# Dilated attention in steps by head, six PSUM banks for a layer's last products, and later sums for the conditions

## The chip, the cores and the metric

The kernel runs on one core of a Trainium2 chip. The metric is the time of one execution on the device in microseconds, taken as the median of several runs. The core has TensorE (PE; PEld is its weight load), VectorE (DVE), ScalarE (ACT), GpSimd (POOL), and SyncE (SP), which issues the DMAs. Each engine executes its instructions in the order in which they were written, and waits in that order too. TensorE writes its products into PSUM, which the kernel divides into eight banks.

## The reference, cut to what matters

A transformer of two blocks with two layers each works on 256 latent tokens of width 1024 (and, in the first block, on 256 context tokens beside them), in float32. Shift, scale and gate vectors of all layers come from condition vectors by `silu(c) @ ada_w + ada_b`. The first block's layer 0 is a retention mixer and a SwiGLU feed-forward on all 512 tokens, its layer 1 a neighbourhood attention and a feed-forward. Each layer of the second block is feed-forward, hybrid mixer, feed-forward:

```python
f = swiglu_2(modulate_2(rmsnorm(h, ln_ffn1[l]), sh1, sc1), ffn1_wg[l], ffn1_wu[l], ffn1_wd[l])
h = h + MACARON_WEIGHT * gt1[:, None, :] * f
u = modulate_2(rmsnorm(h, ln_mix[l]), sh2, sc2)
m = hybrid_mixer(u, ...)
...
def hybrid_mixer(...):
    o_a = gated_delta_rule(q, k, v, g, beta)      # 8 heads of 128, after a convolution
    y_a = o_a @ w_a
    for window, dilation in ((128, 1), (512, 4), (2048, 16)):
        o_p, lse_p = dilated_window_branch(qd, kd, vd, slopes, window, dilation)   # 12 heads of 64
    o_b = sum of the branches' outputs, weighted by softmax over their log-denominators
    y_b = o_b @ w_b
    merged = sigmoid(gate_a) * y_a + sigmoid(gate_b) * y_b
    return merged @ w_o
```

## The kernel before, in words

Every product with a weight matrix is made in three float32r matmuls: the weight tile `w_raw` arrives by DMA, ACT copies its high part (`w_hi`, line `hi`), DVE subtracts it for the low part (`w_lo`), and PE adds high times high, high times low and low times high (`ah`, `al`, `hh`, `hl`, `v_hi`, `v_lo` are the two parts of the activations). A product on 256 tokens has matmuls of 256 columns, one of layer 0 of 512.

The order of all instructions on all engines is fixed when the program is built: it is the order in which the Python code issues them. The code keeps an estimated clock for each engine (`Times`); `b.clock` is PE's. A **side** is a generator that runs beside the main products: after each group of matmuls `b.run` calls `pump`, which lets sides take steps. A side that must be done is run to its end by `finish`, with nothing of the main products between its steps. The sides in a hybrid mixer are the convolution, the delta-rule recurrence ("chain", `delta`, tiles `d_...`), the decays, the condition vectors (`ada_gen`, on DVE) and the dilated attention (`dilated`).

`dilated` treats six pairs of heads through `b.pipeline`, a list of stages. Before the change `first` makes the scores of two heads (8 matmuls from `da_k`, `da_q` into two `ps_tr` banks) and for each head adds the slope (DVE, `da_dist`), takes two maxima (DVE, `da_st`) and two exponentials (ACT); `normalize` multiplies by the number of branches that see a key and sums (DVE, `da_mult`), inverts (DVE) and scales (ACT), again for both heads; `second(0)` and `second(1)` transpose one head each (3 matmuls) and copy it out (ACT: `n_t`, `da_pt`); `third` multiplies with the values (12 matmuls on `sb`) and splits the result (`ah` on ACT, `al` on DVE). The score tile is `n_a` in the trace. A stage is taken when its input and bank are estimated to be there. A stage's fourth entry, where it is given, is a number of microseconds: the stage is then taken only when DVE's estimated work reaches no further than that past PE's clock. The mixer writes its second gate into the memory of the values (`sb`), so the evacuation `gate_b(i)` calls `da.finish()` for i of 1 and above.

There are six PSUM banks for products (`ps_acc` four, `ps_mm` two) and two for the rest (`ps_tr`). `bank(many)` gives one of the six, whichever is free first, if `many` is true, and one of the two of `ps_mm` otherwise. In layer 0 the products `outp` of the retention and `down` of the feed-forward add to the residual `h` in their evacuation on DVE; where they are the layer's last, the evacuation also prepares the following norm (subtraction of `n_piv` on DVE, squares on ACT, sums on POOL, at last sums over partitions by PE into `ps_tr` and `ps_acc`).

`ada_gen` adds up a condition's product on DVE (`ada_acc`, 8 steps for each half), turns and reduces it (`ada_t`, `ada_part`) and puts it on `pending`; `reduce_one` then makes one small matmul with `fold` into `ps_tr` and two DVE operations. The vectors are also forced by `need`, when a product asks for them.

All helpers record one line, L75, so the tiles' names tell the operations apart. The line numbers that the change touches: `ada_gen` 434, `outp` 1269, the layer's `ffn` 1349 with `down` at 1381, and `dilated` 2093.

## Time and profile before

| | |
|---|---|
| time, median of 3 runs (lowest to highest) | 2873.59 us (2870.81 to 2875.27) |
| profiled execution: time / span | 2875.96 us / 2874.1 us |
| mean granted TensorE clock | 0.977 of full |
| busy: PE / PEld / DVE / ACT / POOL | 97% / 89% / 73% / 46% / 10% |
| chain that ended last | PE 82%, DVE 8%, ACT 4%, issue 3% |

The profile shows one execution. "Busy" is the time in which an engine executes; what it waited for is inferred from semaphores. The granted clock of a stretch is a mean: 1.0 is 2.4 GHz, and the lower of its two levels, 1.2 GHz, is 0.5. The chain is followed back from the last instruction, at each step to what released it. 1560 to 1880 us is about the first hybrid mixer, 2310 to 2630 the second; layer 0 of the first block ends at about 890.

### The profile page before, as it was taken

How to read it: one execution, taken by the hardware profiler on the slowest of the kernel's cores; microseconds unless marked ns; L12 is line 12 of the kernel's file. 1: busy time of each engine (PE TensorE's matmuls, PEld its weight loads, DVE VectorE, ACT ScalarE, POOL GpSimd, SP SyncE). 2: the span in 40 equal slices, each digit the busy share in tenths (PEclk: the TensorE clock that was granted, in tenths of full speed). 3: DMA queues.
4: the chain of work that ended last, by engine and by line, in shares of the span. 5: the costliest groups of instructions: out<-in, count | busy, mean ns of one | idle time of the engine just before them, and what ended most of it. 6: DMA issues, size and time to landing. Idle time of an engine off the chain costs nothing.

```text
span 2874.1 us, 49237 instructions
## 1 busy us (share of the span) xinstructions
PE 2776.9 (97%) x19349; PEld 2548.0 (89%) x19349; DVE 2097.7 (73%) x3396; ACT 1322.0 (46%) x2318; POOL 290.0 (10%) x363
## 2 busy tenths in 40 slices
PE   8999998999998998998999989999999999999999
PEld 4878887888877778998999989999999998899999
DVE  5888886887877776787877777788565577676754
ACT  4433323422224544444445665554454456655543
POOL 0000002000002100001002123210010022130100
PEclk9999998999998998998999999999999999999999
DMA  7444441576755543775886533458566654324564
GB/s 232 155 129 144 141 154 63 190 234 211 239 180 144 122 149 117 253 255 157 267 261 199 155 92 115 147 173 273 186 181 184 186 172 118 89 82 153 179 183 133
DMA packets 433245, 488.34 MB, mean 170 GB/s; under 512 B 34651, under 2 KB 362301, under 8 KB 433013
## 3 DMA queue, kind: packets, MB, share of 16 engines
q1 hardware_dynamic: 431972, 484.59, 54.1%
q8 instruction: 152, 2.49, 0.4%
q10 hardware_dynamic: 1040, 0.60, 0.1%
q14 instruction: 81, 0.66, 0.1%
HBM read 484.07 MB, written 1.05 MB: 169 GB/s over the span
## 4 chain that ended last, share of the span: by engine, by line
PE 82%; DVE 8%; ACT 4%; issue 3%; DMA 1%; SPq 1%; POOL 1%; ACTq 0%; DVEq 0%; POOLq 0%
PE ps_acc L75 46%; PE ps_mm L75 32%; PE ps_tr L75 4%; DVE w_lo L75 2%; ACT w_hi L75 2%; DVE n_t L75 1%; DMA ada_w<-ada_w 1%; ACT n_a L75 1%; DVE n_a L75 1%; DVE h L75 1%; DVE al L75 1%; SPq L75 1%; DVE ada_acc L75 0%; DVE da_st L75 0%; ACT ah L75 0%
## 5 line engine op out<-in xcount | busy, mean ns | idle before, releaser
L75 DVE TENSOR_TENSOR w_lo<-w_raw,w_hi 128x1024 fp32r<-128x1024 f32 (+1 forms) x672 | 816.5, 1226 | 426.5 <-ACT w_hi L75 420.8
L75 ACT ACTIVATE w_hi<-w_raw 128x1024 fp32r<-128x1024 f32 (+2 forms) x686 | 699.7, 1032 | 490.3 <-PE ps_acc L75 233.9
L75 PE MATMUL ps_mm<-ah,w_hi 128*128 128x256 f32 (+1 forms) x2288 | 707.0, 309 | 8.1 <-DVE q_lo L75 3.0
L75 PE MATMUL ps_mm<-ah,w_lo 128*128 128x256 f32 (+1 forms) x2288 | 680.8, 298 | 4.0 <-POOL w_lo L75 2.3
L75 PE MATMUL ps_mm<-al,w_hi 128*128 128x256 f32 (+1 forms) x2288 | 681.7, 298 | 0.2
L75 PEld LDWEIGHTS ps_mm<-ah,w_hi 128*128 128x128 f32 x2288 | 434.9, 190 | 31.4 <-issue 11.1
L75 PEld LDWEIGHTS ps_mm<-ah,w_lo 128*128 128x128 f32 x2288 | 435.2, 190 | 18.9 <-POOL w_lo L75 3.4
L75 PEld LDWEIGHTS ps_mm<-al,w_hi 128*128 128x128 f32 x2288 | 435.7, 190 | 12.4 <-DVE al L75 1.0
L75 PE MATMUL ps_acc<-ah,w_hi 128*128 128x256 f32 (+2 forms) x1440 | 436.4, 303 | 2.3 <-ACT w_hi L75 2.3
L75 PE MATMUL ps_acc<-ah,w_lo 128*128 128x256 f32 (+2 forms) x1440 | 433.5, 301 | 1.4 <-DVE w_lo L75 1.3
L75 PE MATMUL ps_acc<-al,w_hi 128*128 128x256 f32 (+2 forms) x1440 | 433.3, 301 | 0.0
L75 DVE SCALAR_TENSOR_TENSOR ada_acc<-ada_w,cact,ada_acc 128x512 f32<-128x512 f32 x476 | 354.4, 759 | 16.8 <-DMA ada_w<-ada_w 11.8
L75 PEld LDWEIGHTS ps_acc<-ah,w_lo 128*128 128x128 f32 x1440 | 274.7, 191 | 12.5 <-DVE w_lo L75 2.6
L75 PEld LDWEIGHTS ps_acc<-ah,w_hi 128*128 128x128 f32 x1440 | 274.5, 191 | 12.2 <-ACT w_hi L75 2.5
L75 PEld LDWEIGHTS ps_acc<-al,w_hi 128*128 128x128 f32 x1440 | 274.8, 191 | 9.6
L75 PE MATMUL ps_acc<-hh,w_hi 128*128 128x256 f32 (+1 forms) x866 | 255.5, 295 | 0.0
L75 PE MATMUL ps_acc<-hh,w_lo 128*128 128x256 f32 (+1 forms) x866 | 255.2, 295 | 0.0
L75 PE MATMUL ps_acc<-hl,w_hi 128*128 128x256 f32 (+1 forms) x866 | 254.9, 294 | 0.0
L75 POOL TENSOR_TENSOR n_a<-n_a 128x512 f32<-128x512 f32 (+1 forms) x28 | 40.4, 1444 | 1292.6 <-ACT n_a L75 1292.1
L75 PEld LDWEIGHTS ps_acc<-hh,w_hi 128*128 128x128 f32 x866 | 163.2, 188 | 4.4
L75 PEld LDWEIGHTS ps_acc<-hl,w_hi 128*128 128x128 f32 x866 | 163.2, 188 | 4.4
L75 PEld LDWEIGHTS ps_acc<-hh,w_lo 128*128 128x128 f32 x866 | 163.0, 188 | 4.4
(391 smaller groups left out, 4368.5 us busy)
## 6 DMA issues: line engine op xcount, KB each, us to landing
ada_w<-ada_w SPq DMA_DIRECT2D x448, 256.0 KB
w_raw<-w_in SPq DMA_DIRECT2D x132, 512.0 KB
w_raw<-ffn_w SPq DMA_DIRECT2D x128, 512.0 KB
w_raw<-ffn_wg SPq DMA_DIRECT2D x88, 512.0 KB
w_raw<-ffn_wu SPq DMA_DIRECT2D x88, 512.0 KB
w_raw<-ffn_wd SPq DMA_DIRECT2D x80, 512.0 KB
w_raw<-ret_w_in SPq DMA_DIRECT2D x48, 512.0 KB
w_raw<-na_w_qkv SPq DMA_DIRECT2D x24, 512.0 KB
```

Source lines behind the costliest of these rows:

```text
L75: r = f(*args, **kw)
```

## The change

Three edits. (1) `ada_gen` takes the reduction of a finished condition only when its input is estimated to be written, not only when a `ps_tr` bank is free. (2) The last retention product and the last part of layer 0's feed-forward may use all six banks. (3) In `dilated`, `first` ends with the slope; maxima and exponentials are a stage `soft(i)` for each head, and `normalize(i)` is one for each head. `first`, `soft` and `normalize` carry 1.0 us as the fourth entry, so that they are taken only when DVE is estimated at most 1.0 us behind PE. The limits are the same ones with the new stage numbers.

```diff
@@ ada_gen
                         while len(self.pending) > 1:
-                            if not self.force and self.free("ps_tr", self.BANKS["tr"]) > self.clock:
+                            when = max(self.free("ps_tr", self.BANKS["tr"]),
+                                       self.times.when(self.times.written, self.pending[0][2]))
+                            if not self.force and when > self.clock:
                                 yield WAIT
@@ outp
-            return b.gemm_b(self.o[h], ..., 512, self.residual(gates, norms), ks=4, many=norms is None)
+            return b.gemm_b(self.o[h], ..., 512, self.residual(gates, norms), ks=4, many=True)
@@ ffn
-                           self.residual(gates, self.norms if part == NP - 1 else None), ks=2 * (f1 - f0), many=part < NP - 1))
+                           self.residual(gates, self.norms if part == NP - 1 else None), ks=2 * (f1 - f0), many=True))
@@ dilated
                 nc.vector.scalar_tensor_tensor(s, dist, slope, ps[:, :384], op0=OP.mult, op1=OP.add)
-                st = P.tile([128, 2, 4], F32, name="da_st", bufs=4)
+                S[n].append((s, P.tile([128, 2, 4], F32, name="da_st", bufs=4)))
+
+        def soft(i):
+            def f(n):
+                s, st = S[n][i]
                 for t, (a, z) in enumerate(segs):
                     nc.vector.tensor_reduce(st[:, t, 0:1], s[:, a:z], axis=AX.X, op=OP.max, negate=True)
                 for t, (a, z) in enumerate(segs):
                     nc.scalar.activation(s[:, a:z], s[:, a:z], AF.Exp, bias=st[:, t, 0:1])
-                S[n].append((s, st))
-
-        def normalize(n):
-            for s, st in S[n]:
+            return f
+
+        def normalize(i):
+            def f(n):
+                s, st = S[n][i]
...
-        stages = ((first, lambda: "tr2", (3, lambda: 2)), (normalize, None, None), (second(0), tr, (4, lambda: 1)), (second(1), tr, None),
-                  (third, tr, None))
+        stages = ((first, lambda: "tr2", (6, lambda: 2), 1.0), (soft(0), None, None, 1.0), (soft(1), None, None, 1.0),
+                  (normalize(0), None, None, 1.0), (normalize(1), None, None, 1.0), (second(0), tr, (7, lambda: 1)),
+                  (second(1), tr, None), (third, tr, None))
```

No instruction is added or removed on any engine; the order changes. Three places follow, each with the rows of the order before and of the order after the change. A row is one instruction (xN: N alike in a row), its outputs and inputs.

ScalarE in the first hybrid mixer, before: exponentials and scalings of `dilated` (`n_a<-n_a,da_st`, two to a head) around copies of weights.

```order
L75 ACTIVATE w_hi<-w_raw 128x1024
L75 ACTIVATE n_a<-n_a,da_st 128x128
L75 ACTIVATE n_a<-n_a,da_st 128x256
L75 ACTIVATE n_a<-n_a,da_st 128x128
L75 ACTIVATE n_a<-n_a,da_st 128x256
L75 ACTIVATE n_a<-n_a,da_st 128x128
L75 ACTIVATE n_a<-n_a,da_st 128x256
L75 ACTIVATE n_a<-n_a,da_st 128x128
L75 ACTIVATE n_a<-n_a,da_st 128x256
L75 ACTIVATE d_XX<-ps_acc 128x256
L75 ACTIVATE cv_x<-ps_mm 128x512
```

The same engine where `dilated` takes its first steps after the change.

```order
L75 ACTIVATE d_t_14769<-ps_acc 128x256
L75 ACTIVATE n_a<-n_a,da_st 128x128
L75 ACTIVATE n_a<-n_a,da_st 128x256
L75 ACTIVATE n_a<-n_a,da_st 128x128
L75 ACTIVATE n_a<-n_a,da_st 128x256
L75 ACTIVATE w_hi<-w_raw 128x1024
L75 ACTIVATE d_XX<-ps_acc 128x256
```

Eight such operations stood between `w_hi` and the chain's `d_XX`; here four stand in a row between a chain copy (`d_t`) and the next `w_hi`.

TensorE in the first hybrid mixer, before, at an end of a pair (`n_t,sb` and `da_pt,sb` are `third`, `ident,n_a` is `second`).

```order
L75 MATMUL ps_tr<-n_t,sb 64x128
L75 MATMUL ps_tr<-da_pt,sb 64x128
L75 MATMUL ps_tr<-ident,n_a 128x128 x3
L75 MATMUL ps_mm<-ah,w_hi 128x256
L75 MATMUL ps_mm<-al,w_hi 128x256
L75 MATMUL ps_mm<-ah,w_lo 128x256
```

TensorE after the change where the evacuation of the second gate forces `dilated` to its end. `da_k,da_q` is `first`.

```order
L75 MATMUL ps_mm<-ah,w_lo 128x256
L75 MATMUL ps_tr<-ident,n_a 128x128 x6
L75 MATMUL ps_tr<-da_k,da_q 128x128 x2
L75 MATMUL ps_tr<-da_k,da_q 128x256 x2
L75 MATMUL ps_tr<-n_t,sb 64x128
L75 MATMUL ps_tr<-da_pt,sb 64x128
```

One or two steps of `dilated` stood between products (`ps_mm`). Now the run goes on behind the last row in the same way through pairs 3, 4 and 5: in all it holds `second` for pairs 2 to 5, `first` for 4 and 5 and `third` for 2 to 5, with no product and no chain step between; in the second hybrid mixer a like run holds `first` for 4 and 5, `second` for 3 to 5 and `third` for 2 to 5. Before, while `dilated` ran, no stretch without a product held half as many matmuls.

VectorE in the last part of layer 0's feed-forward, before: evacuations `h<-ps_mm` of one weight tile's products, the low part of the next weights, and the condition sums.

```order
L75 SCALAR_TENSOR_TENSOR h<-ps_mm,v_lat_0_5_2933,h 128x256
L75 SCALAR_TENSOR_TENSOR h_67<-ps_mm,v_ctx_0_5_3446,h_67 128x256
L75 SCALAR_TENSOR_TENSOR h<-ps_mm,v_lat_0_5_2933,h 128x256
L75 TENSOR_TENSOR h<-h,n_piv 128x512
L75 SCALAR_TENSOR_TENSOR h_67<-ps_mm,v_ctx_0_5_3446,h_67 128x256
L75 TENSOR_TENSOR h_67<-h_67,n_piv 128x512
L75 TENSOR_TENSOR w_lo<-w_raw,w_hi 128x1024
L75 SCALAR_TENSOR_TENSOR ada_acc<-ada_w,cact,ada_acc 128x512 x2
L75 TENSOR_TENSOR w_lo<-w_raw,w_hi 128x1024
```

The same rows after the change (`h_67` is the context's part of the residual in both).

```order
L75 SCALAR_TENSOR_TENSOR h<-ps_acc,v_lat_0_5_2933,h 128x256
L75 SCALAR_TENSOR_TENSOR h_67<-ps_acc,v_ctx_0_5_3446,h_67 128x256
L75 SCALAR_TENSOR_TENSOR h<-ps_acc,v_lat_0_5_2933,h 128x256
L75 TENSOR_TENSOR h<-h,n_piv 128x512
L75 SCALAR_TENSOR_TENSOR h_67<-ps_acc,v_ctx_0_5_3446,h_67 128x256
L75 TENSOR_TENSOR h_67<-h_67,n_piv 128x512
L75 TENSOR_TENSOR w_lo<-w_raw,w_hi 128x1024
L75 SCALAR_TENSOR_TENSOR ada_acc<-ada_w,cact,ada_acc 128x512
L75 TENSOR_TENSOR w_lo<-w_raw,w_hi 128x1024
```

The evacuations read another bank, and one of the two `ada_acc` steps ahead of the next `w_lo` has moved further down.

## Rows read from the trace of the kernel before

**Rows 1.** Page, part 1: busy time of each engine, share of the span, instructions
```profile
PE 2776.9 (97%) x19349; PEld 2548.0 (89%) x19349; DVE 2097.7 (73%) x3396; ACT 1322.0 (46%) x2318; POOL 290.0 (10%) x363
```

**Rows 2.** TensorE's waits, whole span: engine, tile, releaser: us in total, times, longest
```profile
PE ps_acc L75 <- DVE d_MQ L75: 9.7, 2, 4.8
PE ps_mm L75 <- DVE h L75: 9.4, 4, 3.9
...
PE ps_tr L75 <- DVE ada_part L75: 3.2, 3, 2.7
```

**Rows 3.** Stretches: length, busy us (x) of PE, PEld, DVE, ACT, POOL; PEclk, DMA
```profile
860.00:870.00 10.00, 6.12 (x18) 4.68 (x17) 8.25 (x11) 2.21 (x3) 4.88 (x4) 0.66 0.52 160
1610.00:1740.00 130.00, 119.61 (x995) 112.52 (x994) 97.80 (x243) 83.03 (x209) 26.95 (x38) 0.97 0.38 114
1670.00:1680.00 10.00, 5.16 (x28) 4.96 (x27) 6.83 (x24) 5.40 (x13) 1.27 (x2) 0.73 0.18 53
1860.00:1870.00 10.00, 9.05 (x63) 9.00 (x64) 6.40 (x10) 2.43 (x3) 0.57 (x1) 0.83 0.39 130
2360.00:2510.00 150.00, 139.51 (x1169) 132.60 (x1168) 106.05 (x257) 97.15 (x243) 31.38 (x47) 0.98 0.37 110
```

**Rows 4.** Timeline, scores in the first hybrid: start, us, operation, [idle before <-releaser]
```profile
1671.28 1.54 ACT L75 ACTIVATE n_a<-n_a,da_st 128x128 f32<-128x128 f32 x4 [0.82 <-DVE da_st L75]
...
1673.80 1.23 DVE L75 TENSOR_TENSOR w_lo<-w_raw,w_hi 128x1024 fp32r<-128x1024 f32 x1 [1.81 <-ACT w_hi L75]
...
1675.27 0.87 DVE L75 SCALAR_TENSOR_TENSOR d_MQ<-ps_acc,d_st,d_XX 128x256 f32<-128x256 f32 x2
...
1675.81 1.22 PE L75 MATMUL ps_acc<-d_XX,d_t 128*128 128x128 f32 x4 [4.84 <-DVE d_MQ L75]
```

**Rows 5.** Groups on VectorE in 1610 to 1740: xcount | busy us, mean ns
```profile
L75 DVE SCALAR_TENSOR_TENSOR n_a<-n_a,da_mult 128x128 f32<-128x128 f32 (+1 forms) x24 | 8.4, 388 | 0.0
L75 DVE TENSOR_REDUCE da_st<-n_a 128x1 f32<-128x128 f32 (+1 forms) x24 | 7.3, 347 | 0.4
L75 DVE SCALAR_TENSOR_TENSOR n_a<-da_dist,ps_tr 128x384 f32<-128x384 f32 x12 | 6.6, 547 | 0.0
```

**Rows 6.** Groups on ScalarE in the same stretch
```profile
L75 ACT ACTIVATE n_a<-n_a,da_st 128x128 f32<-128x128 f32 (+1 forms) x48 | 19.1, 453 | 14.5 <-DVE da_st L75 14.5
...
L75 ACT ACTIVATE n_t<-ps_tr 128x384 f32<-128x384 f32 x6 | 3.0, 496 | 0.2
...
L75 ACT ACTIVATE ah<-ps_tr 128x256 fp32r<-128x256 f32 x6 | 2.3, 391 | 1.1 <-PE ps_tr L75 1.0
```

**Rows 7.** Timeline on TensorE: two starts in a row after one step's matmuls
```profile
1655.86 0.49 PE L75 MATMUL ps_tr<-ident,n_a 128*128 128x128 f32 x3
...
1656.11 0.36 PE L75 MATMUL ps_mm<-ah,w_hi 128*128 128x256 f32 x1
...
1660.59 0.93 PE L75 MATMUL ps_tr<-da_k,da_q 64*128 64x128 f32 x8
...
1661.45 0.39 PE L75 MATMUL ps_mm<-ah,w_hi 128*128 128x256 f32 x1
```

**Rows 8.** Timeline, end of the recurrence in the first hybrid
```profile
1860.95 0.52 PE L75 MATMUL ps_acc<-ident,d_MT 128*128 128x128 f32 x2 [2.14 <-DVE d_MT L75]
```

**Rows 9.** Timeline, last part of the 512-token layer's feed-forward
```profile
864.11 0.77 PE L75 MATMUL ps_mm<-hh,w_hi 128*128 128x512 f32 x1 [3.88 <-DVE h L75]
...
867.85 1.82 DVE L75 TENSOR_TENSOR w_lo<-w_raw,w_hi 128x1024 fp32r<-128x1024 f32 x1 [1.65 <-ACT w_hi L75]
...
869.59 3.48 DVE L75 SCALAR_TENSOR_TENSOR ada_acc<-ada_w,cact,ada_acc 128x512 f32<-128x512 f32 x2
...
879.01 0.41 PE L75 MATMUL ps_tr<-ada_part,fold 128*128 128x32 f32 x2 [0.28 <-DVE ada_part L75]
```

**Rows 10.** Timeline, last retention output product
```profile
471.76 0.47 PE L75 MATMUL ps_mm<-v_hi,w_hi 128*128 128x512 f32 x1 [3.66 <-DVE h L75]
...
475.50 1.82 DVE L75 TENSOR_TENSOR w_lo<-w_raw,w_hi 128x1024 fp32r<-128x1024 f32 x1 [1.65 <-ACT w_hi L75]
```

More of the change, by code (lines that the diff above doesn't have):

```diff
@@ L1271, in outp @@
             gates = {cn: b.need(cn, (1, 0, 2)) for cn in ("lat", "ctx")}
-            return b.gemm_b(self.o[h], lambda k: (yh[:, k, :], yl[:, k, :]), 512, self.residual(gates, norms), ks=4, many=norms is None)
+            return b.gemm_b(self.o[h], lambda k: (yh[:, k, :], yl[:, k, :]), 512, self.residual(gates, norms), ks=4, many=True)
         raws = [whole(m) for m in (b.nm["tt"], b.nm["all"][:, 0:2])]
@@ L2129, in normalize @@
                     nc.scalar.activation(s[:, a:z], s[:, a:z], AF.Copy, scale=st[:, t, 2:3])
+            return f
         def second(i):
```

## The prediction

> **What bounds the kernel now.** I read the page first: TensorE is busy for 2776.9 us of a span of 2874.1 [rows 1]. The chain that ended last runs mostly over it. So only two things can move the time: the 97 us in which TensorE waits, and stretches in which it runs at the lower of its two clock levels. Next I read its list of waits, to see which of the 97 us lie where the change works. Two waits on the recurrence's `d_MQ` make 9.7 us, four on an evacuation `h` 9.4, three on a condition's `ada_part` 3.2 [rows 2]. The stretch views then price a place as a whole: TensorE is idle for 130 - 119.61 = 10.4 us while dilated attention runs in the first hybrid mixer, and for 150 - 139.51 = 10.5 us in the second [rows 3].
>
> The timelines say why. At 1675.81 TensorE had waited 4.84 us for `d_MQ` on VectorE. `d_MQ` came only at 1675.27, behind a `w_lo` that had itself waited 1.81 us for ScalarE's `w_hi`, and ScalarE was scaling scores (`n_a`, four in 1.54 us from 1671.28) ahead of that copy [rows 4]. So two heads' worth of score work, issued in one piece, sits in front of the weights' copies and of the recurrence, and behind TensorE's wait stand products whose weights are ready. The granted clock of 1670 to 1680 is 0.73 [rows 3]: with levels of 1 and 0.5, (1 - 0.73) / 0.5 = 54% of it at the lower level. The matmuls behind the wait are the ones that pay, some 2.5 us with those of the next stretch. Thus some 13 us is what score work costs in a mixer now, 26 in both.
>
> **Part 3, dilated attention by head: what it can give.** Pieces of half the length, taken only while VectorE is little behind, let `w_hi`, `w_lo` and `d_MQ` come in between. All of the 26 us can go; but VectorE's and ScalarE's sums stay, VectorE is busy for 97.8 and ScalarE for 83.0 of the 130 us [rows 3], and the recurrence is taken faster in the new order, so that more of its dependent steps fall on each product. Its other waits are then next. I take half, -13 us, from -4 to -26.
>
> **Part 3: what it costs.** The steps now begin later and are held back by the 1.0 us, while the place at which they must be done stays: the second gate's evacuation needs the memory of the values. The order shows the outcome. In the first mixer TensorE gets `second` of pairs 2 to 5, `first` of 4 and 5 and `third` of 2 to 5 in one run, without a product or a chain step between. Everything that is behind the gate on TensorE's queue, the next products and the chain, stands behind this run. What hid the score work, products on TensorE, is gone there, so its dependences are bare: scores, slope, maximum, exponential, weighting, scaling, transpose, copy, product.
>
> I walk through the run in the order of issue, each step starting when its engine and input are free. ScalarE has 26 exponentials and scalings at 0.40 (19.1 / 48) to 0.453, 8 copies at 0.495 and 4 `ah` at 0.39 [rows 6]: 26 x 0.453 + 8 x 0.495 + 4 x 0.39 = 17.3 us. VectorE has 14 weightings at 0.35 (8.4 / 24), 12 maxima at 0.30 (7.3 / 24) and 4 slopes at 0.55 [rows 5], 10.7 us without small ones. On TensorE three transposes hold the engine for 1656.11 - 1655.86 = 0.25 us, `first` for 1661.45 - 1660.59 = 0.86 [rows 7]; `third`, 12 short matmuls, I take at 0.8, by `first`. With a pair's steps overlapped with the next one's as the order allows (pair 4's scores go into pair 2's memory, pair 5's into pair 3's), the walk gives from the first transpose: `first` of 4 at 2.5 us, `third` of 2 at 4.8, `first` of 5 at 6.1, `third` of 3 at 8.8, `second` of 4 at 10.7 and 13.8, its `third` at 16.3, the last one done at 20. VectorE arrives late at it and TensorE's steps in it run partly at half clock: 22 us. TensorE's own work in it is 8 x 0.25 + 2 x 0.86 + 4 x 0.8 = 6.9 us, which is due anyway. After so long an idle stretch the products start at the lower level, as after the 4.84 us wait: 1.5 us more. First mixer: 22 - 6.9 + 1.5 = **+16.6**. The second mixer's run lacks the end of pair 2 (2.5 us, and 0.5 of TensorE's own): 19.5 - 6.4 + 1.5 = **+14.6**. Together +31. Lower bound: ScalarE's sum alone, 17.3 - 6.9 = 10.4, and in the second (22 x 0.453 + 6 x 0.495 + 4 x 0.39) - 6.4 = 8, so +18. Upper bound: the sums of ScalarE and VectorE one behind the other, 28 - 6.9 + 1.5 = 22.6 and some 18, so +40. I take the walk since it follows the dependences.
>
> The chain is further on when the run comes, and ends earlier among the products. Before, TensorE waited 2.14 us for its last steps at 1860.95 [rows 8], and the stretch behind has a granted clock of 0.83 [rows 3], so 3.4 us at half rate, 1.7 lost. With the chain earlier I take -2 of these 3.8, from 0 to -3.8.
>
> **Part 2, six banks.** In the last part of the feed-forward TensorE waits 3.88 us at 864.11 for an evacuation to free one of two banks [rows 9], and 860 to 870 has a granted clock of 0.66 [rows 3]; wait and clock together are worth 6 us. But VectorE, which makes the evacuations, is busy for 8.25 of these 10 us [rows 3]. TensorE would run ahead and then wait at the norm's sums for the same last evacuation. What VectorE can pull in is its own wait of 1.65 us for `w_hi` at 867.85 and the one of two `ada_acc` (3.48 / 2 = 1.74 us) that the new order takes from in front of the last evacuations [rows 9]: **-3.3**, from -1 to -6. In the last retention product TensorE waits 3.66 us at 471.76. There VectorE's order does not change, and its `w_lo` at 475.50 also waits for a copy [rows 10] which stands behind a square of the evacuated `h`: the evacuations stay where they are, and the sums behind the products wait in place of the products. **0**, from -3.7 to +1.3: the latter if the longer gap ahead of the sums leaves them at half clock.
>
> Were the banks alone the cause, both waits and the slow matmuls behind them would go: 3.88 + 3.66 and about 2 for each clock stretch, 11.5 us instead of 3.3. This is what the Trainium skill ("Perfetto Trace Analysis", section Optimization Strategy) suggests: the same gap repeating on the engine that should be saturated can mean that there is not enough PSUM for the next tile. By the row on VectorE, 8.25 of 10 us, the trace agrees with the gap but only in part with the cause; the case stands below as a rival.
>
> **Part 1, condition sums.** Holding `reduce_one` helps where TensorE waits for `ada_part`: 3.2 us in three, 2.7 of it in one [rows 2]. That one comes on the path forced by `need`, which the edit does not touch, and the order up to it is unchanged. A 0.28 us wait at 879.01 [rows 9] does go, since that reduction moves on into layer 1, among products, where VectorE's result is long there. **-0.3**, from -1 to +1. Elsewhere the order of the neighbourhood part shifts by a few steps: 0, plus or minus 3.
>
> **The sum.** +31 - 13 - 2 - 3.3 - 0.3 = +12.4 us. The profiled execution took 2875.96 us, 2.4 above the median of the runs; against it 2888.4, and in the median 2873.6 + 12.4 = **2886**.
>
> **The rivals.** *The forced run is cheap and the rest is smooth* (faster). One mechanism: the run costs ScalarE's sum only, +18, since the steps of two pairs overlap fully, and every wait of the 26 us goes; with -2 and -3.6 that is -13.6, 2860. For it: ScalarE waits 14.5 us for `da_st` in that stretch already [rows 6] and is free otherwise. Against it: scores for pair 4 need pair 2's memory, so no more than two pairs overlap. It decides once both runs together cost under 26 + 5.6 - 5.7 = 26 us while all waits go. Chance 0.17.
>
> *It cancels.* The run as walked, +31, but the 26 us go entirely: 31 - 26 - 2 - 3.6 = -0.6, 2873. For it: all these waits hang on long pieces of score work, and these are gone. Against it: more chain steps for each product. Chance 0.2.
>
> *Banks were the limit in layer 0.* -11.5 there instead of -3.3: +4.2, 2878. VectorE's load speaks against it; chance 0.05.
>
> *The run is serial and the chain, now denser, waits as much as the scores did.* +40 - 4 - 2 - 3 = +31, 2905. Chance 0.08.
>
> That the edit does not do what it says is not among them, since the order shows all three parts.
>
> **How the numbers follow.** The forecast has 0.5, and its own range is 2878 to 2897. This kernel's runs tell a change from none at about 0.2%, 5.7 us, so 2867.9 to 2879.3 is "same". Faster: 0.17, from the cheap run. Same: 0.2 and 0.05, 0.25. Slower: 0.5 and 0.08, 0.58. For 8 in 10 the range goes from 2863, within the cheap case, to 2904, just under the serial one.
>
> **What the profile after would show.** If right: in each hybrid mixer one stretch of about 20 us in which TensorE is busy for a third, with waits of `ps_tr` on `n_t`, `da_pt` or `n_a`, and a granted clock under 0.8 in it and behind it; the 4.8 us waits on `d_MQ` gone or under 2 us; the wait of 2.1 on `d_MT` smaller. In layer 0 the 3.9 us wait on `h` gone, with a wait ahead of the norm's sums in its place, and their start 3 us earlier in the feed-forward, no earlier in the retention. It is wrong if the forced stretch is under 15 us, or if TensorE is idle in the rest of these mixers for as long as before or not at all.

## The result

The changed kernel takes 2901.18 us (median of 4 runs, 2898.51 to 2903.47) against 2874.24 before (4 runs, 2870.81 to 2875.27): a ratio of 1.0096, 95% interval 1.0078 to 1.0113. It is 27 us slower. The forecast was 2886, 12.4 us slower: the right sign, but less than half of the size. The time lies inside the range for 8 in 10 (2863 to 2904) and outside the forecast's own range (2878 to 2897). The profiled execution after took 2898.51 us, 22.6 more than that of before; it is the shortest of its four, so terms read from the two traces add up to 22.6 and not to 27.

The page after, busy time of the engines and the chain that ended last by engine:

```profile
PE 2790.2 (96%) x19349; PEld 2549.5 (88%) x19349; DVE 2099.1 (72%) x3396; ACT 1323.1 (46%) x2318; POOL 292.7 (10%) x363
...
PE 80%; DVE 10%; ACT 6%; issue 2%; DMA 1%; SPq 1%; POOL 0%; ACTq 0%; DVEq 0%; POOLq 0%
```

Against [rows 1] the span grew by 22.6 us, TensorE's busy time by 13.3. The work is the same, so 13.3 us of the growth is matmuls that take longer in the records, and only 9.3 us is more idle time. Longer can mean the lower clock level, or a step that stands alone: busy time runs to a step's modelled end, and three transposes count 0.49 us though the next product starts 0.25 us after them [rows 7]. TensorE's waits over the whole span (engine, tile, releaser: us in total, times, longest):

```profile
PE ps_tr L75 <- ACT n_a L75: 16.4, 13, 3.9
PE ps_acc L75 <- ACT d_t L75: 7.0, 9, 2.2
...
PE ps_tr L75 <- ACT n_t L75: 3.3, 6, 0.6
...
PE ps_acc L75 <- ACT d_vb L75: 3.1, 1, 3.1
```

The two waits of 4.8 us on `d_MQ` and the two near 3.8 on `h` [rows 2, 9, 10] are gone. In their place stand waits of `ps_tr` for the scores (`n_a`, `n_t`), and chain steps that wait for ScalarE (`d_t`, `d_vb`).

Where the time went, by stages. Each norm of the program ends with one small POOL operation (`n_st`), whose start marks the same point in every trace. From one such mark to the next, us:

| from, to | before | after | difference |
|---|---|---|---|
| start to the norm after the retention | 485.9 | 485.1 | -0.8 |
| to the end of layer 0 (its feed-forward) | 397.5 | 394.1 | -3.4 |
| first block's layer 1 and the following feed-forward | 646.5 | 640.9 | -5.6 |
| first hybrid mixer | 387.8 | 406.0 | +18.2 |
| two feed-forwards | 381.0 | 381.0 | 0.0 |
| second hybrid mixer | 378.8 | 393.7 | +14.9 |
| from there to the end | 196.6 | 195.9 | -0.7 |

The two mixers, in stretches before, in and behind the forced run (length; busy us (x) of PE, PEld, DVE, ACT, POOL; PEclk; DMA):

```profile
1520.00:1770.00 250.00, 233.35 (x1913) 224.39 (x1912) 188.19 (x400) 147.92 (x370) 72.72 (x107) 0.99 0.44 134
1770.00:1797.00 27.00, 18.75 (x90) 11.36 (x88) 12.85 (x56) 14.66 (x41) 1.32 (x2) 0.59 0.05 15
1797.00:1926.00 129.00, 126.88 (x1061) 125.94 (x1062) 93.90 (x159) 64.75 (x125) 15.50 (x19) 0.99 0.56 179
2307.00:2538.00 231.00, 219.99 (x1828) 212.58 (x1827) 166.64 (x351) 140.62 (x338) 60.22 (x91) 0.99 0.42 124
2538.00:2563.00 25.00, 17.45 (x95) 10.99 (x93) 11.82 (x56) 13.88 (x41) 1.78 (x4) 0.60 0.05 16
2563.00:2701.00 138.00, 135.79 (x1140) 133.83 (x1139) 87.12 (x161) 71.30 (x155) 24.57 (x34) 1.00 0.44 133
```

The run is the stretch at 1770: 27 us with a granted clock of 0.59, a DMA share of 0.05, and TensorE "busy" for 18.75 us with work that holds it for 6.9 at full rate by the prediction's estimate. Outside it TensorE is idle for (250 - 233.35) + (129 - 126.88) = 18.8 us, and in the second mixer for 11.0 + 2.2 = 13.2. The two whole mixers before, same columns:

```profile
1530.00:1918.00 388.00, 368.60 (x3063) 357.63 (x3061) 289.71 (x606) 225.55 (x534) 87.04 (x129) 0.99 0.46 142
2299.00:2677.00 378.00, 363.88 (x3049) 353.84 (x3048) 264.74 (x564) 225.22 (x534) 84.29 (x128) 0.99 0.42 126
```

388 - 368.6 = 19.4 and 378 - 363.9 = 14.1 us. So hardly any idle time went outside the runs: 1.5 us in the two mixers.

### The profile page after: what moved, and what is told of

Read it like the earlier page. It is cut to its first block, busy times and chain, and to the rows that moved or that the text cites. A ratio compares the mean times of both kernels' runs of the same rounds, so it can differ in the third digit from the quotient of the medians.

```text
span 2896.7 us, 49239 instructions
## 1 busy us (share of the span) xinstructions
PE 2790.2 (96%) x19349; PEld 2549.5 (88%) x19349; DVE 2099.1 (72%) x3396; ACT 1323.1 (46%) x2318; POOL 292.7 (10%) x363
## 3 DMA queue, kind: packets, MB, share of 16 engines
q8 instruction: 152, 2.49, 0.3%
## 4 chain that ended last, share of the span: by engine, by line
PE 80%; DVE 10%; ACT 6%; issue 2%; DMA 1%; SPq 1%; POOL 0%; ACTq 0%; DVEq 0%; POOLq 0%
PE ps_acc L75 45%; PE ps_mm L75 30%; PE ps_tr L75 5%; DVE w_lo L75 3%; ACT w_hi L75 2%; DVE n_t L75 1%; ACT n_a L75 1%; DMA ada_w<-ada_w 1%; DVE n_a L75 1%; DVE h L75 1%; DVE al L75 1%; SPq L75 1%; DVE ada_acc L75 1%; DVE d_XX L75 1%; ACT n_t L75 0%
## 5 line engine op out<-in xcount | busy, mean ns | idle before, releaser
L75 PEld LDWEIGHTS ps_mm<-ah,w_lo 128*128 128x128 f32 x2288 | 432.1, 189 | 18.8 <-POOL w_lo L75 3.0
L75 PEld LDWEIGHTS ps_mm<-al,w_hi 128*128 128x128 f32 x2288 | 432.8, 189 | 12.5 <-DVE al L75 0.9
L75 DVE SCALAR_TENSOR_TENSOR ada_acc<-ada_w,cact,ada_acc 128x512 f32<-128x512 f32 x476 | 353.3, 756 | 13.1 <-DMA ada_w<-ada_w 8.5
L75 PEld LDWEIGHTS ps_acc<-ah,w_lo 128*128 128x128 f32 x1440 | 274.6, 191 | 13.2 <-DVE w_lo L75 3.3
L75 PE MATMUL ps_acc<-hh,w_hi 128*128 128x256 f32 (+1 forms) x890 | 265.0, 298 | 0.0
L75 PE MATMUL ps_acc<-hh,w_lo 128*128 128x256 f32 (+1 forms) x890 | 264.4, 297 | 0.0
L75 PE MATMUL ps_acc<-hl,w_hi 128*128 128x256 f32 (+1 forms) x890 | 264.3, 297 | 0.0
```

Source lines behind the costliest of these rows:

```text
L75: r = f(*args, **kw)
```

## The experiments

All are compared with runs of the kernel before on the same chip, whose medians lay between 2874.18 and 2874.87.

**E1, without the dilated part.** `dilated` as before the change, the other two parts as after it.

> Dilated attention as before the change, the six banks and the held condition sums as after it. In the changed kernel the norms up to the end of the first block come 0.8, 4.2, 8.1, 9.5 and 9.8 us earlier than before, and the two hybrid mixers take 18.2 and 14.9 us longer. Theory (the two mixers lose by the forced run alone, the rest of the change is a gain): 9.8 us faster than before, about 2864.5, and mixers as long as before. By the terms of the prediction (-3.3 and -0.3) only 2870. Rival (the early gain is an effect of the dilated part's order, or chance): no difference from before.

Measured: 2865.40 us, ratio 0.9967 (0.9954 to 0.9980), as the theory has it. The two mixers take 386.6 and 380.0 us, about as before (387.8 and 378.8). So the first parts are a gain of some 9 us, and the dilated part costs 2901.2 - 2865.4 = 36 us, more than the whole change.

**E2, split by head but not held back.**

```diff
-        stages = ((first, lambda: "tr2", (6, lambda: 2), 1.0), (soft(0), None, None, 1.0), (soft(1), None, None, 1.0),
-                  (normalize(0), None, None, 1.0), (normalize(1), None, None, 1.0), ...
+        stages = ((first, lambda: "tr2", (6, lambda: 2), None), (soft(0), None, None, None), (soft(1), None, None, None),
+                  (normalize(0), None, None, None), (normalize(1), None, None, None), ...
```

> The whole change, but without the 1.0 us that holds first, soft and normalize back: dilated attention is split by head and no forced run is left in the order. Theory (the hold-back makes the forced run, and that is the loss): faster than before by the early 9.8 us and by 0 to 13 us of the waits on score work, 2851 to 2865. Rival (the split itself, with score steps among denser chain steps, is the loss): the two mixers stay some 15 us each longer than before, 2885 or more.

Measured: 2873.42 us, ratio 0.9996 (0.9986 to 1.0005). Neither number: the forced run is gone and 27.8 us with it, but the split by head alone is 8 us slower than no split (E1), where the prediction had a gain of 13. All of that lies in the first mixer, 394.0 against 386.6 us; the second takes 379.2 against 380.0. TensorE's waits in the first mixer:

```profile
PE ps_acc L75 <- ACT d_t L75: 10.4, 7, 3.1
PE ps_acc L75 <- ACT d_XX L75: 5.4, 6, 2.4
```

The waits on `d_MQ` are gone here too, but the chain now waits for its copies on ScalarE. What ScalarE itself waited for in that mixer:

```profile
ACT n_a L75 <- DVE da_st L75: 35.5, 17, 5.8
```

Before, ScalarE waited 14.5 us for `da_st` [rows 6], here 35.5. Each stage `soft(i)` or `normalize(i)` holds a step on VectorE and the one on ScalarE behind it. Taken with VectorE behind, the step on ScalarE stands in the queue and waits, and the copies queued behind it wait as well. TensorE's longest wait of that mixer is of this kind:

```profile
1721.19 1.49 ACT L75 ACTIVATE n_a<-n_a,da_st 128x128 f32<-128x128 f32 x4 [2.66 <-DVE da_st L75]
...
1723.69 0.37 ACT L75 ACTIVATE d_t<-ps_acc 128x256 f32<-128x256 f32 x1
...
1724.20 0.53 PE L75 MATMUL ps_acc<-ident,d_MT 128*128 128x128 f32 x2 [3.12 <-ACT d_t L75]
```

That is 3.1 of the 15.8 us, and it is not so everywhere. The next longest, 2.49 us at 1764.44, stands behind a copy that waited 3.28 us for the chain's own `d_S` on VectorE. And in the second mixer, which lost nothing, ScalarE waits nearly as long:

```profile
ACT n_a L75 <- DVE da_st L75: 29.2, 14, 5.8
```

So ScalarE's wait for scores costs only where a copy that TensorE needs is queued behind it; its sum does not tell the loss.

**E3, held back but not split.** Two-head stages as before, with the 1.0 us on `first` and `normalize`.

```diff
-        stages = ((first, lambda: "tr2", (3, lambda: 2)), (normalize, None, None), ...
+        stages = ((first, lambda: "tr2", (3, lambda: 2), 1.0), (normalize, None, None, 1.0), ...
```

> The six banks, the held sums, and dilated attention in two-head stages as before, but held back by 1.0 us: the order has forced runs of 48 and 29 matmuls on TensorE where the changed kernel has 58 and 55. Theory (hold-back makes the loss): the loss of 33 us in the two mixers shrinks about with the runs, 33 x 77 / 113 = 22, so 22 - 9.8 = 12 us slower than before, about 2886, from 2880 to 2892. Rival (the split is the loss): 2864, as without the dilated part.

Measured: 2893.32 us, ratio 1.0060 (1.0045 to 1.0075), 28 us above E1. A little over the range of the theory, far from the rival: the hold-back is slow with whole pairs as with heads.

**E4, the six banks alone.**

> Only the six banks in the two last products of layer 0. Theory: the gain up to the end of layer 0, 4.2 us, is theirs and the further 5.6 us up to the end of the first block belong to the held condition sums: 2870, and the norms behind layer 0 stay 4.2 us early. Rival (what follows is an effect of the banks too): 2864.

Measured: 2864.22 us, ratio 0.9956 (0.9939 to 0.9972). The rival's number: all of the gain up to the end of the first block comes with the banks, in layer 0 by 3.5 us (397.5 to 394.0) and in the next stage by 4.1 (646.5 to 642.4), in which the planner's order shifts with them. The size of the second is not settled by one trace. The changed kernel, E1, E2 and E5 have the same order on TensorE, VectorE and ScalarE from the end of layer 0 to the next norm, and this stretch still takes 226.1 to 231.7 us in them, against 233.6 before and 233.3 in E12, which has no six banks.

**E5 and E6, matmuls for the clock.** In the forced runs (and at one forced `first` ahead of them in each mixer) eight (E5) or four (E6) matmuls that nobody reads, ahead of each `first`, `second` and `third`:

```diff
+        def warm():
+            if b.force:
+                for i in range(8):
+                    if i % 2 == 0:
+                        d = b.psum.tile([128, 512], F32, name="ps_acc", bufs=4)
+                    nc.tensor.engine.matmul(d[:, 0:128], b.ident, b.ident, start=True, stop=True)
...
         def third(n):
+            warm()
             ps = b.ps("tr")
```

> The changed kernel, with eight more matmuls of 128 columns (identity by identity, into a bank nobody reads) ahead of each first, second and third stage in the forced runs, 14 times in the first mixer and 12 in the second; the order is else the same. In the changed kernel the runs last 27.0 and about 24 us, with the granted clock at 0.5, against 22 and 19.5 in the prediction. Theory (the runs are longer than walked since TensorE's own steps in them are made at the lower level): with the engine kept busy the clock stays up and the runs come down to 21 to 23 and 19 to 20, 7 to 9 us in all, 2893. Rival (ScalarE and VectorE set the length, and the clock does nothing): the runs stay as long or get longer by what of the 26 x 0.9 = 22 us does not fit into the gaps, 2901 to 2915.

> As e5_warm8, with four such matmuls each time, about 11 us in the two runs. Theory: where the clock stays up as in e5_warm8, the same gain or some more, 2890 to 2895; where four do not keep it up, no gain and up to 11 us of loss. Rival (the clock does nothing): 2901 to 2908.

Measured: E5 2916.65 us, ratio 1.0143 (1.0128 to 1.0158); E6 2899.22, 1.0080 (1.0064 to 1.0097), against 2901.18 (1.0096) without them. E5 is just beyond its rival's range, E6 between theory and rival. E5 keeps TensorE busy for the whole run and makes it longer: 33.6 us in the first mixer, from its first idle matmul on. E6, stretches in its run (columns as above):

```profile
1780.00:1790.00 10.00, 8.87 (x75) 7.63 (x77) 4.67 (x20) 6.35 (x17) 0.00 (x0) 1.00 0.10 34
1790.00:1800.00 10.00, 8.56 (x76) 7.03 (x73) 5.86 (x28) 5.91 (x16) 0.00 (x0) 1.00 0.01 2
```

The granted clock is 1.00, where the changed kernel has 0.59 over its run. The run from its first transpose to the first chain step behind it, E6:

```profile
1778.57 0.49 PE L75 MATMUL ps_tr<-ident,n_a 128*128 128x128 f32 x3
...
1803.20 0.71 PE L75 MATMUL ps_acc<-d_XX,d_MT 128*128 128x128 f32 x4
```

1803.20 - 1778.57 = 24.6 us, against 27.0 in the changed kernel (below), though 13 of the groups of four stand in it, some 1 us each (the one ahead of the first transpose from 1777.58 to 1778.57). In the second mixer it is 21.9 against 23.9. So a run at the upper level is 2.0 to 2.4 us shorter even with these matmuls in it. The kernel gains no more than 2.0 us by the medians: a group stands ahead of each run too, and in this trace the first mixer is 1.9 us longer than in the changed kernel, the second 2.4 shorter. That the level explains all of the 5 us between walk and run isn't shown by this.

**E7, held back by 2.0 us.** The number 1.0 replaced by 2.0 throughout.

> The whole change, with a hold-back of 2.0 instead of 1.0 us. The order has one forced run of 22 matmuls in the first mixer and none in the second. Theory (what costs is the forced run, not the hold-back itself): near the kernel with no hold-back (2873), with some 3 us for the short run, 2873 to 2878. Rival (late score steps cost by themselves): 2885 or more.

Measured: 2882.28 us, ratio 1.0025 (1.0016 to 1.0035). Between theory and rival. The second mixer, with no forced run, is as long as before (378.5 us). The first, with one of 22 matmuls that lasts only 7.9 us, is 404.6, nearly as in the changed kernel (406.0). ScalarE waits 29.4 us for `da_st` there, 12.6 in the second, and TensorE waits 8.5 us in the first for the chain's `d_XX` from ScalarE. So a forced run is not the only harm. That the waiting score steps are the other fits these numbers and isn't shown by them.

**E8, only weighting and scaling by head, not held back.**

```diff
+        stages = ((firstboth, lambda: "tr2", (4, lambda: 2)), (normalize(0), None, None), (normalize(1), None, None), (second(0), tr, (5, lambda: 1)),
+                  (second(1), tr, None), (third, tr, None))
```

> Six banks and held sums, dilated attention without hold-back and with only the weighting and scaling split by head (scores, maxima and exponentials of two heads in one stage as before). With no split 2865.4 was measured, with both split 2873.4. Theory (each more piece of score work among the chain's copies delays some of them on ScalarE): about half of the 8 us, 2868 to 2871. Rival (the split of the exponentials alone does it): 2865; or the split of the scaling alone: 2873.

Measured: 2886.90 us, ratio 1.0041 (1.0026 to 1.0056). Slower than with both split, which none of the three cases allowed: the pieces don't add up one by one. ScalarE in the first mixer:

```profile
ACT n_a L75 <- DVE da_st L75: 25.8, 16, 4.1
```

Here too it is well above the 14.5 of before; in the second mixer it is 25.0. The mixers take 399.7 and 387.5 us.

**E9 and E10, stages by engine.** If waiting score steps on ScalarE are the trouble, each engine's step should be a stage of its own, so that the one on ScalarE is issued only when the one on VectorE is estimated done. E9 does it for two heads at once, E10 with exponentials, weighting and scaling also by head; neither is held back. E10's stages (`top` takes the maxima, `exps` the exponentials, `weigh` multiplies and sums, `scale` scales):

```diff
+        one = lambda n: (first(n), top((0, 1))(n))
+        stages = ((one, lambda: "tr2", (8, lambda: 2)), (exps((0,)), None, None), (exps((1,)), None, None), (weigh((0,)), None, None),
+                  (scale((0,)), None, None), (weigh((1,)), None, None), (scale((1,)), None, None),
+                  (second(0), tr, (9, lambda: 1)), (second(1), tr, None), (third, tr, None))
```

> Six banks and held sums; dilated attention without hold-back and not by head but by engine: scores and maxima, exponentials (ScalarE), weighting (VectorE), scaling (ScalarE), each a stage for two heads, so that ScalarE gets a score step only when the step on VectorE before it is estimated done. No forced run in the order. Theory (the recurrence's copies wait on ScalarE behind score steps that themselves wait for VectorE): these waits go, the 4.8 us waits with them, and the time falls below the 2865.4 of the two other parts, 2852 to 2862. Rival (ScalarE's and VectorE's work on the scores is itself the delay, whatever its order): 2863 to 2875.

> As e9_by_engine, and exponentials, weighting and scaling by head as well. Theory (waiting score steps in front of the copies): as e9 or a little better, 2850 to 2862. Rival (each further piece only moves the waits): 2870 to 2887, as the two kernels split by head without forced run (2873.4 and 2886.9).

Measured: E9 2871.72 us, ratio 0.9989 (0.9979 to 0.9998), 6 above E1 and in the rival's range; E10 2853.03 us, ratio 0.9922 (0.9907 to 0.9937), in the theory's range, 12 below E1 and 21.6 below the kernel before. In both ScalarE's wait for `da_st` is gone from the mixers; what is left of it in E10's first:

```profile
ACT n_a L75 <- DVE da_st L75: 0.3, 1, 0.3
```

TensorE's waits in the first mixer, E9 and then E10:

```profile
PE ps_acc L75 <- DVE d_MQ L75: 2.8, 1, 2.8
```

```profile
PE ps_acc L75 <- DVE d_XX L75: 3.6, 4, 1.5
PE ps_acc L75 <- ACT d_XX L75: 2.3, 4, 1.4
```

In E9 one wait for `d_MQ` remains in each mixer, 2.8 and 2.2 us. In the first, `d_MQ` stands on VectorE behind slopes and maxima of two heads (1.0 and 1.1 us) and three steps of the convolution (1.5 us). E10 has no such wait, though its slopes and maxima are taken for two heads as well. E9's mixers take 387.2 and 382.6 us, no less than E1's 386.6 and 380.0: the whole of ScalarE's wait for `da_st`, 14.5 us in a mixer, went without a gain. So taking the waiting score steps off ScalarE is not enough, nor are short pieces (E2); E10 has both and gains.

**E11, late pairs.** E1's kernel, with pairs 4 and 5 not begun until the gate forces them.

```diff
-        yield from b.pipeline(6, stages, lambda n: n // 2 in self.qk, begun)
+        yield from b.pipeline(6, stages, lambda n: n // 2 in self.qk and (n < 4 or b.force), begun)
```

> Six banks and held sums, dilated attention in two-head stages without hold-back, but pairs 4 and 5 are not begun until the second gate's evacuation forces them: runs of 36 and 35 matmuls, and the other four pairs where they were. Theory (a forced run costs its bare dependences less TensorE's own steps): some 14 us for two pairs, less 4.3 of own work, with 2 for the clock, 12 in each mixer, less 1 to 4 for the waits that the two pairs no longer cause earlier, so 16 to 22 us over 2865.4, 2881 to 2887. Rival (not the run but the delay of all score steps costs): 2864 to 2870.

Measured: 2890.98 us, ratio 1.0057 (1.0042 to 1.0072), 25.6 above E1. The theory's mechanism, a little dearer: two pairs in a forced run cost 12.5 us in each mixer (399.1 and 392.4 us against 386.6 and 380.0). TensorE's waits in the first:

```profile
PE ps_acc L75 <- DVE d_MQ L75: 4.8, 1, 4.8
PE ps_tr L75 <- ACT n_a L75: 3.4, 1, 3.4
```

The wait on `d_MQ` of before is there as it was, and the wait for `n_a` is the run's.

**E12, the held condition sums alone.**

> Only the held condition sums. With both first parts 2865.4 was measured, with the banks alone 2864.2, before 2874. Theory (the banks make all of that gain, the sums nothing that can be told): 2872 to 2876. Rival (in layer 1 the sums gain some 4 us, as the norms' times suggest): 2868 to 2871.

Measured: 2874.32 us, ratio 0.9999 (0.9989 to 1.0008). No difference, as the theory has it.

**E13, E10's stages held back by 1.0 us.**

> The stages of e10_by_engine_head (2853.0) held back by 1.0 us as in the change. The order has forced runs of 79 and 49 matmuls where e10 has none and the changed kernel has 58 and 55. Theory (the hold-back costs through the forced run alone, some 28 us for 58 and 55): 2853 + 28 to 40, 2881 to 2893. Rival (with the stages by engine the hold-back does no harm): 2850 to 2860.

Measured: 2898.06 us, ratio 1.0067 (1.0043 to 1.0092), 45 above E10, somewhat over the theory's range: the forced runs of 79 and 49 matmuls (34.2 and 18.2 us in the trace) undo far more than the better stages give. The run in the first mixer (columns as above):

```profile
1770.00:1780.00 10.00, 8.79 (x46) 6.02 (x46) 4.30 (x13) 3.06 (x8) 0.00 (x0) 0.50 0.00 0
1780.00:1790.00 10.00, 6.70 (x30) 3.67 (x26) 3.94 (x23) 6.42 (x18) 0.00 (x0) 0.50 0.01 2
```

**E14, the maxima by head as well.**

> As e10_by_engine_head, with the maxima taken out of the scores' stage and made a stage for each head too, without hold-back. In the order the chain gets ahead again and a short run of 22 matmuls is forced in the second mixer. Theory (shorter pieces on VectorE help, as by head against two heads): 2845 to 2852. Rival (the short forced run eats it): 2853 to 2862.

Measured: 2866.53 us, ratio 0.9969 (0.9959 to 0.9980). 13.5 us slower than E10, outside both ranges. The rival's reason is not enough either: the short run in the second mixer lasts 4.4 us. ScalarE's wait for `da_st` is 1.1 us over both mixers, so that isn't the cause. The first mixer, which has no forced run, is 7 us longer than in E10 (386.2 against 379.0) and the second 10 (382.9 against 373.2); the waits are on `d_vb` and `d_st`, steps of the chain. Why this order lets the chain wait more was not traced. With short pieces and next to no waiting scores on ScalarE it still has no gain over E1 (2865.4), so the two together don't ensure one.

**E15, E10 without the held sums.**

> e10_by_engine_head without the held condition sums, which alone made no difference (2874.3 against 2874.6): the same time as e10, 2849 to 2857. Rival (the sums gain a few us in layer 1, hidden so far): 2857 to 2862.

Measured: 2851.95 us, ratio 0.9917 (0.9901 to 0.9932): the same as E10, so the sums do nothing beside it either. This is the best version found, 22.9 us faster than before on the same chip.

## Why the prediction was right or wrong, point by point

**Part 2 in layer 0: the right number, and half of the reason.** -3.3 was predicted for the feed-forward, -3.4 measured, and 394.0 to 394.1 us in every kernel with the six banks. The wait that was to take the place of the wait on `h` is there. Timeline after, at the end of that feed-forward (as [rows 9] before; all marks here lie 0.75 us earlier by what came before):

```profile
866.58 1.84 DVE L75 TENSOR_TENSOR w_lo<-w_raw,w_hi 128x1024 fp32r<-128x1024 f32 x1 [1.65 <-ACT w_hi L75]
...
867.22 1.84 PE L75 MATMUL ps_tr<-ones,n_a 128*128 128x1 f32 x16
...
868.34 1.75 DVE L75 SCALAR_TENSOR_TENSOR ada_acc<-ada_w,cact,ada_acc 128x512 f32<-128x512 f32 x1
...
869.60 0.61 PE L75 MATMUL ps_acc<-ones,n_a 128*128 128x1 f32 x4 [0.54 <-POOL n_a L75]
...
871.26 2.72 PE L75 MATMUL ps_acc<-ones,n_a 128*128 128x1 f32 x12 [1.06 <-POOL n_a L75]
...
874.24 0.63 ACT L75 ACTIVATE n_a<-h 128x512 f32<-128x512 f32 x1 [6.75 <-DVE h L75]
...
874.92 1.01 PE L75 MATMUL ps_tr<-ones,n_a 128*128 128x1 f32 x4 [0.46 <-ACT n_a L75]
```

TensorE no longer waits for `h`; its first sums begin at 867.22, and it then waits 0.54 and 1.06 us for POOL's part of the norm; VectorE has one `ada_acc` of 1.75 us ahead of the last evacuations, where there were two. But the two terms of the -3.3 did not come as they were added. The 1.65 us that `w_lo` waits for `w_hi` are still there, at 866.58, and the next `w_lo` takes 2.28 us where it took 1.23. The square of the last evacuations begins at 874.24, before at 876.32, so 1.3 us earlier beyond the common 0.75. The rest is on TensorE, before:

```profile
876.32 0.63 ACT L75 ACTIVATE n_a<-h 128x512 f32<-128x512 f32 x1 [3.20 <-DVE h L75]
...
879.25 0.95 PE L75 MATMUL ps_tr<-ones,n_a 128*128 128x1 f32 x4
```

There the square ended at 876.95 and TensorE, still at earlier sums and two condition sums (`fold`, the second at 879.01 [rows 9]), took it 2.3 us later. After, it takes it 0.05 us after its end. So 1.3 us came from VectorE and some 2.2 from TensorE no longer being late; that they add up to the forecast is luck. The Trainium skill ("Perfetto Trace Analysis", section Optimization Strategy) takes a repeated gap for a possible lack of PSUM: the runs agree as to the gap, which six banks remove, but of the 11.5 us that it would make in layer 0 by that reading 3.4 came.

In the retention's last product, timeline after (as [rows 10]):

```profile
473.67 0.60 PE L75 MATMUL ps_tr<-ones,n_a 128*128 128x1 f32 x4 [1.36 <-POOL n_a L75]
474.14 1.79 DVE L75 TENSOR_TENSOR w_lo<-w_raw,w_hi 128x1024 fp32r<-128x1024 f32 x1 [1.64 <-ACT w_hi L75]
...
474.90 2.72 PE L75 MATMUL ps_tr<-ones,n_a 128*128 128x1 f32 x12 [0.62 <-POOL n_a L75]
```

VectorE's `w_lo` waits 1.64 us for its copy as before, TensorE waits 1.36 and 0.62 us for POOL ahead of the sums, and the sums behind run slowly (12 in 2.72 us). The predicted 0 stands beside a measured -0.8, which is within what the start of the program varies by: the same mark lies at 484.7 to 488.7 us in the experiments' traces. With it the bank rival, -11.5 in layer 0, fell. That the banks alone give 10.0 us in the whole kernel (E4) is near its number by another way, the stage behind.

**Layer 1: 0 plus or minus 3 was wrong.** E4's trace has -4.1 there and the one after -5.6; over all traces the stage takes 636.5 to 644.8 us with the six banks, 646.0 and 646.4 without. So the sign is clear and the size is not. The order shifts with the banks, but which waits it spares there stays open: I had not looked, and the terms had no place for such a gain. **Part 1: right**, by -0.3 predicted and nothing measured (E12).

**Part 3, the forced runs: right mechanism, term too small.** +31 was predicted. The run in the first mixer, timeline after:

```profile
1769.91 0.49 PE L75 MATMUL ps_tr<-ident,n_a 128*128 128x128 f32 x3
...
1773.01 0.84 PE L75 MATMUL ps_tr<-ident,n_a 128*128 128x128 f32 x3 [2.61 <-ACT n_a L75]
...
1774.47 0.48 PE L75 MATMUL ps_tr<-da_k,da_q 64*128 64x128 f32 x2 [0.62 <-ACT n_t L75]
...
1776.80 1.02 DVE L75 SCALAR_TENSOR_TENSOR n_a<-da_dist,ps_tr 128x384 f32<-128x384 f32 x2 [2.09 <-PE ps_tr L75]
...
1781.26 2.35 PE L75 MATMUL ps_tr<-da_k,da_q 64*128 64x128 f32 x8
...
1788.33 1.09 PE L75 MATMUL ps_tr<-ident,n_a 128*128 128x128 f32 x3 [1.75 <-ACT n_a L75]
...
1796.89 1.22 PE L75 MATMUL ps_acc<-d_XX,d_MT 128*128 128x128 f32 x4
```

From 1769.91 to 1796.89 it is 27.0 us, where the walk gave 22; in the second mixer 23.9 (2539.36 to 2563.24) against 19.5. With TensorE's own 6.9 and 6.4 us taken off, 20.1 + 17.5 = 37.6, inside the +18 to +40 given for it. The dependences were walked at full rate, with a part of 2 us on top for lateness and clock together. The lateness used that up at once: the walk's `first` of pair 4, at 2.5 us, begins 4.6 us into the run (1774.47), and the granted clock was still 0.99 from 1770 to 1775. From 1775 on it is 0.50, the level of 1.2 GHz, and there the walk was short: `first` takes 2.35 us at 1781.26, against 0.93 in [rows 7], and `third` and the transposes take about twice their time. E6 shows that at least 2.0 to 2.4 us of a run go with the clock. The 1.5 us set for the products behind each run are not in the 37.6; the 10 us behind the runs have a granted clock of 0.91 and 0.98, which is less. E11 gives the same mechanism its own price, 12.5 us for two pairs.

**Part 3, what the split gives back: wrong, the step that failed.** -13 for the waits and -2 for the chain's end were predicted. Idle time outside the runs fell by only 0.6 + 0.9 = 1.5 us, and with the clock around those waits, what remains of +18.2 + 14.9 = 33.1 after the runs, 33.1 - 37.6 = -4.5, is all that came back. The prediction had named this as a sign of being wrong: TensorE idle in the rest of the mixers for as long as before.

The step has two parts. The first is the price of 13 us a mixer. It took all idle time of [rows 3] as the cost of score work, 10.4 us, while [rows 4] tie only the 4.84 us on `d_MQ` to it. The second is that pieces of half the length let `w_hi` and `d_MQ` come in between. They do, and both waits on `d_MQ` went. But other chain steps wait in their place. Summed over the wait lists, TensorE waits for the chain for 14.4 and 11.7 us in the two mixers before, and for 13.1 and 10.4 outside the runs after: 26.1 became 23.5. Of these sums 6.8 us were ended by a copy on ScalarE before and 13.0 after. The prediction had said that the chain's other waits come next, and took half for them without a row; they took nearly all.

The longest of the new waits, timeline after:

```profile
1718.39 2.94 DVE L75 SCALAR_TENSOR_TENSOR n_t<-cv_x,cwT,n_t 128x255 f32<-128x255 f32 x6
...
1722.57 0.37 ACT L75 ACTIVATE d_vb<-ps_acc,d_st 128x128 f32<-128x128 f32 x1 [4.42 <-DVE d_st L75]
...
1722.99 0.49 PE L75 MATMUL ps_acc<-d_k 128*128 128x128 f32 x2 [3.09 <-ACT d_vb L75]
```

No score step is in it: six steps of the convolution (`n_t`) and a `w_lo` of 1.22 us stand on VectorE ahead of the chain's `d_st`, and ScalarE's `d_vb` waits for that. The next in the first mixer, 2.32 us at 1661.67, stands behind the same kind of piece (2.94 us at 1657.22). One in the second, 2.25 us at 2479.29, begins with score steps that wait 1.22 us on ScalarE, as in E2.

In the changed kernel ScalarE waits less for `da_st` than before. The first mixer:

```profile
ACT n_a L75 <- DVE da_st L75: 9.5, 10, 2.4
```

5.0 of the 9.5 us lie ahead of the run. So the coupling of VectorE and ScalarE in one piece, which E2 shows in a wait, is at most a part of what kept the gain small here, and that it does so in general isn't shown: E9 is without it and gains nothing. E2 shows the split without a run: +8 instead of -15. The 14.5 us that ScalarE waits for `da_st` [rows 6], which the prediction read as room for the cheap run, were neither room nor, by E9, a cost by themselves. E10 and E15, with the same work in another order, are 12 and 13 us below E1; that is the most any order here got of the 26.

The cheap-run rival fell (the runs cost more, not less), and so did the one that cancels. The serial one, +31 in all, came nearest in time, with part of its mechanism: the chain waits nearly as much as the scores did, -4.5 against its -4. Its runs, +40, come near the measured 37.6 for another reason, since a part of these is the clock and not one sum behind the other. Its chance of 0.08 was too low: the recovery was taken at the middle of its bounds without a row that speaks for the middle.

The terms beside each other, us:

| term | predicted | from the traces |
|---|---|---|
| forced runs | +31 | +37.6 |
| waits on scores and chain's end | -15 | -4.5 |
| layer 0 (with -0.8 from the start) | -3.3 | -4.2 |
| layer 1 and condition sums | -0.3 | -5.6 |
| sum | +12.4 | +23.3 |

With the -0.7 behind the second mixer this is the 22.6 by which the traces' spans differ; the medians differ by 27, of which the profiled executions show the shorter end.

## What to carry to other kernels

Side work that has a deadline was not made cheaper here by holding it back: what was left at the deadline ran with nothing beside it, and paid its bare dependences at a lowered clock (the changed kernel against E2, E3 and E11 against E1, E13 against E10). Cutting the side work finer is no gain by itself: by head alone it lost 8 us (E2), by engine alone 6 (E9), both together won 12 (E10), and one cut more lost that again (E14). A saving made of waits that another order is to remove counts only for the waits that rows tie to what is removed, and only when one can name what each engine's queue holds next.

## What the runs showed of the hardware

In the changed kernel's first forced run, dependent small matmuls with waits of up to 2.61 us between them, the granted clock fell from 0.99 (1770 to 1775 us) to 0.50, the lower level, and stayed there to the run's end at 1797. With four idle matmuls ahead of each step (E6) it was 1.00 over the whole of the same run (1777.5 to 1803.2). I had expected the run's own steps to keep more of it.
